# Both attentions in pairs of heads, the value product turned round, the weights divided before the transpose

## The chip, the cores and the metric

The kernel runs on one core of a Trainium2 chip. The metric is device time in microseconds (us), lower is better. The engines are called as in the profile: PE is the matrix engine (TensorE), DVE the vector engine, ACT the scalar engine, POOL is GpSimd, SP issues most DMAs. Each engine works through its own queue in a fixed order.

## The reference, cut to what matters

The network has two blocks on 512 tokens of 1024 features. The first block runs a banded attention with a relative bias beside an RWKV recurrence, twice in depth in the reference's loop over its layers; the second has an mLSTM beside a "forgetting" attention, and more layers that this change leaves alone. Both attentions have 8 heads of 64 features and are softmax(scores + bias) times the values:

```
def chunk_band_attention(q, k, v, rel_bias):
    ...
    scores = jnp.einsum('bnqhd,bnkhd->bnhqk', qc, kb).astype(jnp.float32) * (d ** -0.5)
    ...
    scores = jnp.where(valid[None, :, None, None, :], scores + bias[None, None], NEG_INF)
    p = jax.nn.softmax(scores, axis=-1)
    out = jnp.einsum('bnhqk,bnkhd->bnqhd', p.astype(vb.dtype), vb)

def forgetting_attention(q, k, v, f_pre):
    F = jnp.cumsum(jax.nn.log_sigmoid(f_pre.astype(jnp.float32)), axis=-1)
    ...
        logits = jnp.einsum('bhqd,bhkd->bhqk', qb, k).astype(jnp.float32) * scale + fq[..., :, None] - F[..., None, :]
        logits = jnp.where(kpos[None, :] <= qpos[:, None], logits, -jnp.inf)
        p = jax.nn.softmax(logits, axis=-1)
        return jnp.einsum('bhqk,bhkd->bhqd', p.astype(v.dtype), v)
```

## The kernel before

A static scheduler puts the instructions of all stages into one fixed order for each engine; nothing is decided at run time. Most of the work is dense products (`dense_A`, line L163, 128x512 results named psA, and `dense_B`, L281, psB), whose weights stream in by DMA on SP's queue and are split into a high and a low part on ACT (L132) and DVE (L133). The scheduler fills the waits of other stages with such dense products where PSUM banks allow: they live in a pool `mm` of two banks.

The first block's attention (`attention1`, from L1520) works on two halves of four heads each; the second block's (in `layer0`, from L901) does the same. `attention_heads` (L1552) walks units of one head and one query tile t of 128 rows; in unit t the keys have n = 128(t+1) columns. A unit is: the scores (L1569, tile pss; the head's 64 features lie in one row half of PE's array), in the second attention also a causal mask added by a bf16 product (L1571); on DVE the bias added with a running minimum of the negated sum (L1573, into sb); on ACT the exponential with its sum (L1575); t+1 transposes on PE (L1583, pspt); a copy out of PSUM on ACT or DVE in turn (L1586, L1588, pT); and t+1 value products (L1597, pso), which hold a 128x128 piece of pT in the array and move 64 columns of v. After a head's four units the result is multiplied by 1/sum (L1600, L1601), and for two heads together it is transposed to feature rows by `rows_to_T` (L941, psr, four transposes) and split in high and low parts (L318 on ACT, L319 on DVE). PE's order is: scores of unit u, transposes of u-1, values of u-2. PSUM: attention1 has two banks for pss and pspt together, layer0 four; pso has one bank in attention1, two in layer0.

In attention1 the RWKV mixer runs at the same time: during its first half of heads DVE also does the triangular solve (`wk`, L1396 and L1397, 15 dependent steps), during the second half the last recurrence steps (L1450 to L1494) and the group norm (products L1502 and L1506, ACT's logarithm and exponential L1509 and L1511 with a table load each, DVE L1515 and L1516) run.

The lines above are those of the kernel before. Its functions, and those that call them:

Of the kernel before, what the change touches and what calls it, by code (L numbers as in the profile page):

```python
# [17 lines left out]
S = 512  # L18
# [8 lines left out]
# ---- per-feature vectors, features on partitions: name -> number of 128-columns  # L27
# [61 lines left out]
class Halves:  # L89
    """a tile [128, 2, 8, 256] (token half, feature tile, token) as [128 features, 512 tokens] of one feature tile"""  # L90
# [12 lines left out]
class Builder:  # L103
# [155 lines left out]
    def dense_B(self, xk, w, col0, pp, tag="mm", width=512, toks=(0, 1, 2, 3), ps=None, chunks=None, low=None):  # L259
        """x W[:, col0:col0+width], tokens on partitions: {token tile: [128, width] PSUM view}; low: as in dense_A"""  # L260
# [46 lines left out]
    def mix_part(self, xk, w, pp):  # L307
        """column half 0: xN = ALPHA * xN + the part of the mixer's output that is ready"""
# [28 lines left out]
    def to_T(self, xn, n, pair, t, pp, tag, k0=0):  # L337
        """xn: [128 tokens, n*128] -> columns t of pair's tiles k0..k0+n, split"""
# [20 lines left out]
    # ------------------------------------------------------------ row vectors  # L359
# [12 lines left out]
    def rsqrt(self, out, src, n, scale, eps):  # L372
        """out = (scale * src + eps) ** -0.5 on [128, n] columns"""
# [21 lines left out]
    def ln_apply(self, x, st, g, b):  # L395
        """layer norm over 1024 features in place, eps 1e-5; st: bn_stats of the halves"""
# [19 lines left out]
    # ------------------------------------------------------------------ setup  # L416
# [48 lines left out]
    # ---------------------------------------------------------- block 1 mixer  # L465
    def block1_in(self, pool):
# [3 lines left out]
        with ExitStack() as es:  # L470
# [13 lines left out]
            # the tensor engine's clock rises only while it works  # L484
# [308 lines left out]
    def log1pexp_neg_abs(self, out, u):  # L793
        """out = ln(1 + exp(-|u|))"""
# [5 lines left out]
    # ---------------------------------------------------------------- layer 0  # L800
    def layer0(self):
# [3 lines left out]
        with ExitStack() as es:  # L805
            with ExitStack() as es2:
                lp = self.pool(es2, "l0")
                dr = es2.enter_context(self.tc.tile_pool(name="l0d", bufs=1, space=bass.MemoryType.DRAM))
                sel = self.selector(lp, "w", 4)
                one = lp.tile([96, 512], F32, name="one")  # L810
# [5 lines left out]
                # the first two heads' v, and gates: forget rows 0:4 (mLSTM), 32:36 and 64:68 (attention), input rows 96:100  # L816
# [17 lines left out]
                gu = lp.tile([128, 512], F32, name="gu")  # L834
                nc.scalar.activation(gu, pg, AF.Identity, bias=self.p("b_gate"))
                # mLSTM inputs
# [19 lines left out]
                F = lp.tile([96, 512], F32, name="F")  # L856
# [3 lines left out]
                nF = lp.tile([96, 512], F32, name="nF")  # L860
# [4 lines left out]
                cr = lp.tile([32, 512], F32, name="cr")  # L865
# [3 lines left out]
                M = lp.tile([32, 512], F32, name="M")  # L869
                nc.vector.tensor_tensor_scan(M, one[0:32, :], cr, 0.0, op0=ALU.mult, op1=ALU.max)  # L870
                em = lp.tile([32, 512], F32, name="em")
# [3 lines left out]
                # columns by token: c (0:4 of each 64), exp(-m) (32:36)  # L875
# [24 lines left out]
                idb = lb.tile([128, 128], BF16, name="idb")  # L900
                nc.vector.tensor_copy(idb, self.ident)  # L901
                cm = lb.tile([128, 128], BF16, name="cm")
                nc.gpsimd.memset(cm, 0.0)
                nc.gpsimd.affine_select(out=cm, in_=cm, pattern=[[-1, 128]], base=0, channel_multiplier=1, compare_op=ALU.is_ge, fill=NEG)
# [775 lines left out]
```

## Time and profile before

| | |
|---|---|
| median of 3 runs | 2110.13 us (2109.53 to 2110.42) |
| profiled execution, first to last instruction (span) | 2106.5 us |
| runs above that span | 3.0 to 3.9 us |
| PE busy | 2065.2 us (98%) |
| DVE, ACT, POOL busy | 1114.8, 765.6, 163.5 us |
| mean granted clock of PE | 0.995 |

The busy share of PE is a mean over the whole span, and a busy PE is not a PE at its peak: two products that use half of the array each count as busy whether they run one after the other or side by side. How long PE waits, and for whom, is read at each place.

### The profile page before, as it was taken

The numbers are of one execution on the slowest core, as the hardware profiler recorded it, in microseconds if no ns is written. First come the engines' busy times: TensorE is split into PE (matmuls) and PEld (weight loads), VectorE is DVE, ScalarE is ACT, GpSimd is POOL, SyncE is SP. The second block draws the span as 40 slices with busy tenths as digits, with TensorE's granted clock in tenths as the row PEclk, the third lists the DMA queues.
The fourth block names the chain that finished last, engine by engine and source line by source line (L and its number), as shares of the span: only waits on it lengthen the run. The fifth ranks groups of instructions, "written<-read, shape, count | busy, mean of one in ns | idle before, by whom it ended". The sixth has DMA issues, their size and how long they took to land.

```text
span 2106.5 us, 27707 instructions
## 1 busy us (share of the span) xinstructions
PE 2065.2 (98%) x11216; PEld 1696.1 (81%) x11216; DVE 1114.8 (53%) x1831; ACT 765.6 (36%) x1213; POOL 163.5 (8%) x258
## 2 busy tenths in 40 slices
PE   8999999999999999999999999999999999999998
PEld 6678677777888888888777888888897789888886
DVE  4554455565532424544534765435576676543565
ACT  4431552144333423333333344314334534432441
POOL 1101110110000000112200000000020310000000
PEclk9999999999999999999999999999999999999999
DMA  6241125143233334232212322333322033332332
GB/s 205 71 88 42 31 71 107 42 145 104 77 94 100 93 97 125 76 107 80 61 60 91 101 89 91 100 106 109 112 74 80 31 110 101 100 100 90 100 100 91
DMA packets 175120, 192.52 MB, mean 91 GB/s; under 512 B 31560, under 2 KB 144712, under 8 KB 174992
## 3 DMA queue, kind: packets, MB, share of 16 engines
q1 hardware_dynamic: 169920, 173.40, 27.4%
q0 software_dynamic: 5072, 17.35, 2.6%
q8 instruction: 88, 1.44, 0.3%
q14 instruction: 40, 0.33, 0.1%
HBM read 184.94 MB, written 5.78 MB: 91 GB/s over the span
## 4 chain that ended last, share of the span: by engine, by line
PE 53%; DVE 1%; DMA 1%; POOL 1%; ACT 0%; issue 0%; DVEq 0%; ACTq 0%; POOLq 0%
PE psA L163 29%; PE psB L281 19%; PE pss L1569 1%; PE pso L1597 1%; PE pho L1137 1%; DMA raw<-od_w_out 1%; PE psT L345 0%; PE pspt L1583 0%; PE ppg L1176 0%; PE pss L1571 0%; PE pqk L965 0%; PE pho L973 0%; DVE wlo L133 0%; PE psr L941 0%; ACT whi L132 0%
## 5 line engine op out<-in xcount | busy, mean ns | idle before, releaser
L133 DVE TENSOR_TENSOR wlo<-raw,whi 128x1024 fp32r<-128x1024 f32 (+1 forms) x295 | 360.3, 1224 | 506.9 <-ACT whi L132 303.3
L132 ACT ACTIVATE whi<-raw 128x1024 fp32r<-128x1024 f32 (+1 forms) x295 | 311.7, 1056 | 635.7 <-PE psA L163 288.4
L163 PE MATMUL psA<-xTh,whi 128*128 128x512 f32 (+1 forms) x1616 | 416.9, 378 | 3.6 <-ACT xTh L318 1.7
L163 PE MATMUL psA<-xTl,whi 128*128 128x512 f32 (+1 forms) x1616 | 415.8, 377 | 1.3 <-DVE st L375 1.3
L163 PE MATMUL psA<-xTh,wlo 128*128 128x512 f32 (+1 forms) x1616 | 412.1, 376 | 0.0
L163 PEld LDWEIGHTS psA<-xTh,whi 128*128 128x128 f32 x1616 | 288.8, 189 | 59.6 <-issue 3.0
L163 PEld LDWEIGHTS psA<-xTl,whi 128*128 128x128 f32 x1616 | 291.1, 190 | 56.2 <-issue 2.7
L163 PEld LDWEIGHTS psA<-xTh,wlo 128*128 128x128 f32 x1616 | 286.9, 188 | 53.3 <-issue 2.3
L772 DVE SCALAR_TENSOR_TENSOR v<-psA,par,v 128x511 f32<-128x511 f32 (+1 forms) x176 | 131.3, 747 | 78.9 <-ACT v L770 76.5
L376 POOL TENSOR_TENSOR st<-st,mhalf 128x1 f32<-128x1 f32 (+1 forms) x40 | 32.9, 822 | 1266.7 <-DVE st L375 1266.5
L281 PE MATMUL psB<-whi,hidh 128*128 128x512 f32 x480 | 126.7, 390 | 0.0
L281 PE MATMUL psB<-wlo,hidh 128*128 128x512 f32 x480 | 126.4, 389 | 0.0
L281 PE MATMUL psB<-whi,hidl 128*128 128x512 f32 x480 | 126.4, 389 | 0.0
L281 PEld LDWEIGHTS psB<-whi,hidl 128*128 128x128 f32 x480 | 90.1, 188 | 18.8
L281 PEld LDWEIGHTS psB<-wlo,hidh 128*128 128x128 f32 x480 | 90.1, 188 | 18.7
L281 PEld LDWEIGHTS psB<-whi,hidh 128*128 128x128 f32 x480 | 90.0, 188 | 18.7
L770 ACT ACTIVATE v<-psA,par 128x512 f32<-128x512 f32 x88 | 67.8, 771 | 98.0 <-PE psA L163 98.0
L281 PE MATMUL psB<-whi,xTh 128*128 128x256 f32 (+2 forms) x320 | 53.4, 289 | 0.0
L281 PE MATMUL psB<-whi,xTl 128*128 128x256 f32 (+2 forms) x320 | 52.6, 287 | 0.6 <-DVE xTl L319 0.6
L318 ACT ACTIVATE xTh<-psT 128x512 fp32r<-128x512 f32 x40 | 21.9, 595 | 84.2 <-PE psT L345 84.2
L281 PE MATMUL psB<-wlo,xTh 128*128 128x256 f32 (+2 forms) x320 | 49.3, 286 | 0.0
L1575 ACT ACTIVATE sb<-sb,sm 128x128 f32<-128x128 f32 (+1 forms) x64 | 35.7, 559 | 34.1 <-DVE sm L1573 33.5
(406 smaller groups left out, 2503.2 us busy)
## 6 DMA issues: line engine op xcount, KB each, us to landing
raw<-fup SPq DMA_DIRECT2D x88, 512.0 KB, 3.5
raw<-fdn SPq DMA_DIRECT2D x44, 512.0 KB, 3.3
raw<-w_in SPq DMA_DIRECT2D x42, 512.0 KB, 3.8
raw<-w_up SPq DMA_DIRECT2D x32, 512.0 KB, 3.8
raw<-w_down SPq DMA_DIRECT2D x32, 512.0 KB, 3.7
raw<-ev_w_in SPq DMA_DIRECT2D x26, 512.0 KB, 3.7
raw<-od_w_in SPq DMA_DIRECT2D x14, 512.0 KB, 3.8
raw<-w_out SPq DMA_DIRECT2D x8, 512.0 KB, 3.7
```

Of the source, the lines that this page charges most:

```text
L132: i = nc.scalar.activation(hi, raw, AF.Copy)
L133: self.w_ins = (i, nc.vector.tensor_tensor(lo, raw, hi.bitcast(F32), op=ALU.subtract))
L163: i = nc.tensor.matmul(o.rearrange("p (h t) -> p h t", h=2) if len(x.shape) == 3 else o, wt[:, k, fs], x, start=first and half != 1, stop= ...
L281: nc.tensor.matmul(ps[t], xk[k0 + k][a][:, t * 128 : t * 128 + 128], wt[:, k, :], start=first, stop=(end and k == kn - 1 and wt is lo), sk ...
L318: nc.scalar.activation(hi, src, AF.Copy)
L376: return nc.gpsimd.tensor_tensor(out, out, self.mhalf[:, 0:n], op=ALU.pow)
L770: nc.scalar.activation(v, ps[f], AF.Identity, scale=self.p(f"fcw{l}", 88 + ft), bias=self.p(f"fcb{l}", ft))
L772: nc.vector.scalar_tensor_tensor(v[:, sh:], ps[f][:, : 512 - sh], self.p(f"fcw{l}", tap * 44 + ft), v[:, sh:], op0=ALU.mult, op1=ALU.add)
L1137: nc.tensor.matmul(po[:, t, :], w[:, (t - j) * 128 : (t - j) * 128 + 128], xdt[j][:, h * 64 : h * 64 + 64], start=(j == 0 and t == 0), sto ...
L1569: nc.tensor.matmul(ps[:, 0:n], q[hs, t * 128 : t * 128 + 128], k[hs, 0:n], start=True, stop=cmask is None, skip_group_check=True)
L1575: nc.scalar.activation(sb[:, 0:n], sb[:, 0:n], AF.Exp, scale=-1.0, bias=sm[:, t : t + 1], accum_out=sm[:, 4 + t : 5 + t])
L1597: nc.tensor.matmul(po[:, t, :], pT[:, j * 128 : j * 128 + 128], v(j), start=(t == 0 and j == 0), stop=(j == t), skip_group_check=True)
```

## The change

The units are now a pair of heads and a query tile (`attention_pairs`).
- Both heads' scores are issued one behind the other in the two row halves of the array, each into a bank of its own (L1566). The score stage has the same bias and exponential instructions as before, two of each a unit (L1570, L1572).
- The exponentials are multiplied by 1/sum (reciprocal L1579) before they are transposed (L1581): the first head's tile on DVE, the second's on POOL. The multiplication of the result (L1601) is gone.
- The transposes (L1586) go, in attention1, into the two banks of `mm`, which the dense products also use; in layer0 into the four banks of `ax`. The copies are the first head's on ACT (L1589), the second's on DVE (L1591).
- The value product is turned round (L1604): v (128x64) is held, pT moves in 128 columns, and the two heads write the two column halves. The result has features on rows, so `rows_to_T` and its transposes are gone, and the split reads pso.
- The causal mask is put into the bias of the second attention ahead of time: per head four DMAs and four selections on POOL (L906, L908) instead of one DMA, three buffers instead of two. The bf16 mask products are gone.
- The tiles sb and pT of both attentions come from one ring of eight.

```diff
-                def fbias(h):
-                    b = lb.tile([128, 512], F32, tag="fb", bufs=2, name=self.nm("fb"))
-                    nc.gpsimd.dma_start(b, bass.AP(tensor=fd.tensor, offset=fd.offset + h * 512, ap=[[0, 128], [1, 512]]))
-                    return lambda t: b[:, 0 : 128 * (t + 1)]
+                def fbias(h):
+                    b = lb.tile([128, 1280], F32, tag="fb", bufs=3, name=self.nm("fb"))
+                    row = lambda t: b[:, 64 * t * (t + 1) : 64 * (t + 1) * (t + 2)]
+                    for t in range(4):
+                        nc.gpsimd.dma_start(row(t), bass.AP(tensor=fd.tensor, offset=fd.offset + h * 512, ap=[[0, 128], [1, 128 * (t + 1)]]))
+                        d = row(t)[:, t * 128 : t * 128 + 128]
+                        nc.gpsimd.affine_select(out=d, in_=d, pattern=[[-1, 128]], base=0, channel_multiplier=1, compare_op=ALU.is_ge, fill=NEG)
+                    return row
...
+        def scores(u):
+            ...
+            for e in range(2):
+                nc.tensor.matmul(ps[e][:, 0:n], q[hf[e], t * 128 : t * 128 + 128], k[hf[e], 0:n], start=True, stop=True)
+            for e in range(2):
+                b = tt("sb")
+                nc.vector.tensor_tensor_reduce(out=b[:, 0:n], in0=ps[e][:, 0:n], in1=bias[id(pr)][e](t), op0=ALU.add, op1=ALU.min,
+                                               scale=-1.0, scalar=3e38, accum_out=sm[:, e : e + 1])
+                nc.scalar.activation(b[:, 0:n], b[:, 0:n], AF.Exp, scale=-1.0, bias=sm[:, e : e + 1], accum_out=sm[:, 2 + e : 3 + e])
...
+        def weights(u):
+            nc.vector.reciprocal(sm[:, 2:4], sm[:, 2:4])
+            for e in range(2):
+                (nc.vector, nc.gpsimd)[e].tensor_scalar(sb[e][:, 0:n], sb[e][:, 0:n], sm[:, 2 + e : 3 + e], None, op0=ALU.mult)
+            for e in range(2):
+                pt = ptile(self.nm("pspt"))
+                for j in range(n // 128):
+                    nc.tensor.transpose(pt[:, j * 128 : j * 128 + 128], sb[e][:, j * 128 : j * 128 + 128], self.ident)
...
+        def values(u):
+            for j in range(t + 1):
+                for e in range(2):
+                    nc.tensor.matmul(o[hf[e], t * 128 : t * 128 + 128], v(j, e), pT[e][:, j * 128 : j * 128 + 128],
+                                     start=(t == 0 and j == 0), stop=(j == t), skip_group_check=True)
+            if t == 3:
+                self.split(o, *out)
```

How the order moves, at three places. First PE in the first half of attention1's heads, near its start: the rows before (psA are dense products, the numbers behind the names are buffers).

```order
L163 MATMUL psA_1738<-xTh_83,whi_1742 128x512 x4
L163 MATMUL psA_1738<-xTl_84,whi_1742 128x512
L1583 MATMUL pspt_1503<-start,sb_1495 128x128
L163 MATMUL psA_1738<-xTl_84,whi_1742 128x512 x2
L1569 MATMUL pss_1507<-qk_1367,qk_1301 128x384
L1583 MATMUL pspt_1512<-start,sb_1500 128x128 x2
L1597 MATMUL pso_1489<-v_1371,pT_1505 128x64
L163 MATMUL psA_1738<-xTl_84,whi_1742 128x512
```

And the rows of PE at the same place now.

```order
L1566 MATMUL pss_1504<-qk_1367,qk_1301 128x256
L1566 MATMUL pss_1505<-qk_1367,qk_1301 128x256
L1566 MATMUL pss_1526<-qk_1367,qk_1301 128x384
L1566 MATMUL pss_1527<-qk_1367,qk_1301 128x384
L1586 MATMUL pspt_1517<-start,sb_1497 128x128
L1586 MATMUL pspt_1521<-start,sb_1500 128x128
L1586 MATMUL pspt_1539<-start,sb_1508 128x128 x2
L1586 MATMUL pspt_1544<-start,sb_1511 128x128 x2
L1604 MATMUL pso_1549<-pT_1519,v_1371 64x128
```

The dense products that stood between the attention's steps, 39 in this half, now stand behind its last transposes and values. The second half of heads now stands behind the whole recurrence, with only the group norm's four products between its steps, and its 37 dense products stand behind it as well.

Second DVE in the second half of attention1's heads: what stood around the group norm's last four operations (yT) before.

```order
L1515 SCALAR_TENSOR_TENSOR yT_974<-yT_974,par,gsq_976 128x512
L1515 SCALAR_TENSOR_TENSOR yT_975<-yT_975,par,gsq_977 128x512
L1516 SCALAR_TENSOR_TENSOR yT_974<-yT_974,par,bon_574 128x512
L1516 SCALAR_TENSOR_TENSOR yT_975<-yT_975,par,bon_610 128x512
L1601 TENSOR_TENSOR o_1985<-pso_2031,sm_2030 128x4x64
```

And what stands there now.

```order
L1579 RECIPROCAL st_2008<-st_2008 128x2
L1513 SCALAR_TENSOR_TENSOR yT_974<-yT_974,par,gsq_976 128x512
L1513 SCALAR_TENSOR_TENSOR yT_975<-yT_975,par,gsq_977 128x512
L1514 SCALAR_TENSOR_TENSOR yT_974<-yT_974,par,bon_574 128x512
L1514 SCALAR_TENSOR_TENSOR yT_975<-yT_975,par,bon_610 128x512
L1581 TENSOR_SCALAR sb_2013<-sb_2013,st_2008 128x256
```

The multiplication of unit t=1's weights, which that unit's transposes on PE wait for, now stands behind the group norm's four operations.

Third POOL in the first half of the second attention's heads; before, POOL had only the bias DMAs there.

```order
L908 DMA fb_8442<-fd 128x512
L908 DMA fb_8504<-fd 128x512
L908 DMA fb_8845<-fd 128x512
L908 DMA fb_8891<-fd 128x512
```

Now the multiplications L1581 of the second head of each pair stand among the DMAs and selections of the later heads' biases (fb).

```order
L1581 TENSOR_SCALAR sb_8410<-sb_8410,st_8402 128x384
L906 DMA fb_8476<-fd 128x128
L906 DMA fb_8476<-fd 128x256
L906 DMA fb_8476<-fd 128x384
L906 DMA fb_8476<-fd 128x512
L1581 TENSOR_SCALAR sb_8437<-sb_8437,st_8429 128x512
L908 AFFINE_SELECT fb_8476<-fb_8476 128x128 x2
```

The multiplication of the first pair's last unit stands behind four DMA issues. On SP's queue only the place of two weight transfers of the second block's closing product changes.

## Rows read from the trace of the kernel before

**Rows 1.** Windows, only line L163 on PE: start and end, length, busy (count), clock, DMA.

```profile
119.94:156.65 36.71, 13.40 (x39) 1.00 0.47 95
213.19:260.94 47.75, 12.86 (x37) 1.00 0.12 34
1045.86:1080.63 34.77, 9.44 (x27) 1.00 0.16 46
1081.00:1096.00 15.00, 15.00 (x68) 1.00 0.35 106
```

**Rows 2.** Windows, only line L281 on PE, same columns.

```profile
1108.22:1141.00 32.78, 7.58 (x43) 1.00 0.18 57
```

**Rows 3.** Timeline of PE: start, duration, engine, line, operation, tiles, shapes, count.

```profile
1049.94 1.12 PE L1569 MATMUL pss<-k,q 64*128 64x512 f32 x2
...
1051.06 0.61 PE L1597 MATMUL pso<-fv,pT 128*128 128x64 f32 x4
1051.51 0.50 PE L1583 MATMUL pspt<-start,sb 128*128 128x128 f32 x3
1051.94 0.48 PE L1569 MATMUL pss<-k,q 64*128 64x128 f32 x2
...
1052.39 0.71 PE L163 MATMUL psA<-xTl,whi 128*128 128x512 f32 x2
```

**Rows 4.** Timeline of PE, recurrence inside the second attention stretch (first and last of 13).

```profile
214.04 0.43 PE L1488 MATMUL psy<-PR,S 128*128 128x64 f32 x2
...
227.68 0.45 PE L1494 MATMUL psy<-G,VW 128*64 128x64 f32 x8
```

**Rows 5.** Groups of PE by shape, 213 to 261: busy us, mean ns.

```profile
L1502 PE MATMUL psm<-yT,cst 128*128 128x512 f32 x4 | 2.1, 618 | 0.0
```

**Rows 6.** Timeline of PE, products with two row halves of the array.

```profile
103.07 1.32 PE L1369 MATMUL psg<-PR,KB 64*128 64x128 f32 x16
```

**Rows 7.** Groups of DVE by shape, 119.94 to 156.65: busy us, mean ns | idle before.

```profile
L1573 DVE CUSTOM_DVE_ANT_0 sb<-pss,relb 128x512 f32<-128x512 f32 x4 | 2.8, 692 | 2.3 <-PE pss L1569 2.3
...
L1573 DVE CUSTOM_DVE_ANT_0 sb<-pss,relb 128x128 f32<-128x128 f32 x4 | 1.2, 291 | 6.8 <-PE pss L1569 5.6 <-issue 1.2
L1600 DVE RECIPROCAL sm<-sm 128x4 f32<-128x4 f32 x4 | 0.7, 174 | 0.9 <-ACT sb L1575 0.9
```

**Rows 8.** Groups of DVE by line, the same stretch: the two lines of the solve.

```profile
L1396 DVE TENSOR_TENSOR wk<-wk 128x1 f32<-128x1 f32 (+14 forms) x15 | 4.5, 301 | 0.2
...
L1397 DVE TENSOR_REDUCE wk<-wk 128x1 f32<-128x1 f32 (+14 forms) x15 | 3.5, 236 | 0.3
```

**Rows 9.** Timeline of ACT: two exponentials in the second attention.

```profile
1114.65 0.71 ACT L1575 ACTIVATE sb<-sb,sm 128x512 f32<-128x512 f32 x1
...
1115.36 0.39 ACT L1575 ACTIVATE sb<-sb,sm 128x128 f32<-128x128 f32 x1
```

**Rows 10.** Groups of POOL by shape, whole span.

```profile
L1475 POOL TENSOR_SCALAR S<-S,eLC 128x128 f32<-128x128 f32 x24 | 15.6, 659 | 134.2 <-DVE S L1483 91.9 <-DVE S L1481 42.3
...
L1325 POOL TENSOR_TENSOR KB<-ta,eLm 128x512 f32<-128x512 f32 x4 | 5.9, 1483 | 17.1 <-DVE ta L1324 13.4 <-ACT VW L1351 3.7
...
L908 POOL DMA_DIRECT2D fb<-fd x8 | 4.4, 557 | 94.2 <-DVE sm L1573 93.2 <-DMA fd<-nF 1.0
...
L1444 POOL MEMSET gsq<- 128x512 f32 x4 | 2.1, 531 | 0.0
```

**Rows 11.** Timeline of ACT, DVE and PE around the group norm.

```profile
240.13 1.28 ACT L1511 ACT_TABLE_LOAD   x1
...
242.09 1.41 DVE L1515 SCALAR_TENSOR_TENSOR yT<-yT,par,gsq 128x512 f32<-128x512 f32 x2 [2.84 <-ACT gsq L1511]
...
243.28 0.44 PE L1583 MATMUL pspt<-start,sb 128*128 128x128 f32 x2 [1.90 <-ACT pT L1586]
```

**Rows 12.** Windows of 3 us on PE: busy (count), granted clock, DMA.

```profile
1632.00:1635.00 3.00, 1.18 (x5) 1.00 0.14 50
...
1638.00:1641.00 3.00, 3.00 (x9) 0.53 0.01 3
```

More of the change, by code (lines that the diff above doesn't have):

```diff
@@ L807, in layer0 @@
                 lp = self.pool(es2, "l0")
+                tt = lambda n, rows=128: lp.tile([128, 512], F32, tag="t", bufs=8, name=self.nm(n))[0:rows]
                 dr = es2.enter_context(self.tc.tile_pool(name="l0d", bufs=1, space=bass.MemoryType.DRAM))
                 sel = self.selector(lp, "w", 4)
-                one = lp.tile([96, 512], F32, name="one")
+                one = tt("one", 96)
                 nc.gpsimd.memset(one, 1.0)
@@ L855, in layer0 @@
                 self.po = self.pool(es2, "pspo", 2, psum=True)
-                F = lp.tile([96, 512], F32, name="F")
+                F = tt("F", 96)
                 self.log1pexp_neg_abs(F, gu[0:96, :])
@@ L1544, in attention1 @@
                 nc.scalar.activation(v[:, t, :], ps[t], AF.Copy)
-            o = [ap.tile([128, 4, 128], F32, tag="o", bufs=2, name=self.nm("o")) for _ in range(2)]
-            self.attention_heads(ap, [
-                (qk[0][hh // 2], qk[1][hh // 2], hh, lambda j, hh=hh, v=v: v[:, j, hh * 64 : hh * 64 + 64], o[hh // 2],
-                 lambda hh=hh: rbias(4 * hf + hh), None) for hh in range(4)])
-            for f in range(2):
-                self.rows_to_T(o[f], self.ya[0][:, 2 * hf + f, :], self.ya[1][:, 2 * hf + f, :])
@@ L1552, in attention_heads, with attention_pairs @@
-    def attention_heads(self, ap, heads):
+            self.attention_pairs(lambda n: ap.tile([128, 512], F32, tag="t", bufs=8, name=self.nm(n)), [
+                (qk[0][f], qk[1][f], lambda j, e, f=f, v=v: v[:, j, f * 128 + e * 64 : f * 128 + e * 64 + 64],
+                 lambda e, f=f, hf=hf: rbias(4 * hf + 2 * f + e), (self.ya[0][:, 2 * hf + f, :], self.ya[1][:, 2 * hf + f, :]))
+                for f in range(2)], lambda n: mm.tile([128, 512], F32, tag="mm", name=n))
+    def attention_pairs(self, tt, pairs, ptile):
@@ L1555, in attention_heads @@
         nc, at = self.nc, self.at
-        units = [(hd, t) for hd in heads for t in range(4)]
-        st = {}
+        units = [(pr, t) for pr in pairs for t in range(4)]
+        hf = (slice(0, 64), slice(64, 128))
+        st, po, bias = {}, {}, {}
         def scores(u):
-            hd, t = units[u]
-            q, k, h, v, o, biasf, cmask = hd
+            pr, t = units[u]
+            q, k, v, biasf, out = pr
             if t == 0:
-                sm = ap.tile([128, 8], F32, tag="sm", bufs=3, name=self.nm("sm"))
-                st[id(hd)] = (sm, self.po.tile([128, 4, 64], F32, tag="po", name=self.nm("pso")), biasf())
-            sm, po, bf = st[id(hd)]
-            hs = slice((h % 2) * 64, (h % 2) * 64 + 64)
+                bias[id(pr)] = [biasf(e) for e in range(2)]
@@ L1567, in scores @@
             n = 128 * (t + 1)
-            ps = at.tile([128, 512], F32, tag="ax", name=self.nm("pss"))
-            nc.tensor.matmul(ps[:, 0:n], q[hs, t * 128 : t * 128 + 128], k[hs, 0:n], start=True, stop=cmask is None, skip_group_check=True)
-            if cmask is not None:
-                nc.tensor.matmul(ps[:, n - 128 : n], cmask[0], cmask[1], start=False, stop=True, skip_group_check=True)
-            sb = ap.tile([128, 512], F32, tag="sb", bufs=3, name=self.nm("sb"))
-            nc.vector.tensor_tensor_reduce(out=sb[:, 0:n], in0=ps[:, 0:n], in1=bf(t), op0=ALU.add, op1=ALU.min,
-                                           scale=-1.0, scalar=3e38, accum_out=sm[:, t : t + 1])
@@ L1575, in scores @@
-            nc.scalar.activation(sb[:, 0:n], sb[:, 0:n], AF.Exp, scale=-1.0, bias=sm[:, t : t + 1], accum_out=sm[:, 4 + t : 5 + t])
-            st[u] = sb
-        def transposes(u):
-            n = 128 * (units[u][1] + 1)
-            sb = st[u]
-            pt = at.tile([128, 512], F32, tag="ax", name=self.nm("pspt"))
-            for j in range(n // 128):
-                nc.tensor.transpose(pt[:, j * 128 : j * 128 + 128], sb[:, j * 128 : j * 128 + 128], self.ident)
-            pT = ap.tile([128, 512], F32, tag="pT", bufs=2, name=self.nm("pT"))
-            if u % 2 == 0:
-                nc.scalar.activation(pT[:, 0:n], pt[:, 0:n], AF.Copy)
-            else:
-                nc.vector.tensor_copy(pT[:, 0:n], pt[:, 0:n])
-            st[u] = pT
@@ L1591, in values @@
-        def values(u):
-            hd, t = units[u]
-            h, v, o = hd[2:5]
-            sm, po, _ = st[id(hd)]
+            sm = self.stat(4)
+            ps = [at.tile([128, 512], F32, tag="ax", name=self.nm("pss")) for _ in range(2)]
+            for e in range(2):
+                nc.tensor.matmul(ps[e][:, 0:n], q[hf[e], t * 128 : t * 128 + 128], k[hf[e], 0:n], start=True, stop=True)
+            sb = []
+            for e in range(2):
[3 more added lines that the diff above has]
+                nc.scalar.activation(b[:, 0:n], b[:, 0:n], AF.Exp, scale=-1.0, bias=sm[:, e : e + 1], accum_out=sm[:, 2 + e : 3 + e])
+                sb.append(b)
@@ new lines, in scores @@
+            st[u] = (sb, sm)
+        def weights(u):
+            n = 128 * (units[u][1] + 1)
+            sb, sm = st[u]
+            nc.vector.reciprocal(sm[:, 2:4], sm[:, 2:4])
+            for e in range(2):
+                (nc.vector, nc.gpsimd)[e].tensor_scalar(sb[e][:, 0:n], sb[e][:, 0:n], sm[:, 2 + e : 3 + e], None, op0=ALU.mult)
+            row = []
+            for e in range(2):
+                pt = ptile(self.nm("pspt"))
+                for j in range(n // 128):
+                    nc.tensor.transpose(pt[:, j * 128 : j * 128 + 128], sb[e][:, j * 128 : j * 128 + 128], self.ident)
+                pT = tt("pT")
+                if e == 0:
+                    nc.scalar.activation(pT[:, 0:n], pt[:, 0:n], AF.Copy)
+                else:
+                    nc.vector.tensor_copy(pT[:, 0:n], pt[:, 0:n])
+                row.append(pT)
+            st[u] = row
@@ L1595, in values @@
+        def values(u):
+            pr, t = units[u]
+            v, out = pr[2], pr[4]
+            if t == 0:
+                po[id(pr)] = self.po.tile([128, 512], F32, tag="po", name=self.nm("pso"))
+            o = po[id(pr)]
             pT = st.pop(u)
             for j in range(t + 1):
-                nc.tensor.matmul(po[:, t, :], pT[:, j * 128 : j * 128 + 128], v(j), start=(t == 0 and j == 0), stop=(j == t), skip_group_check=True)
+                for e in range(2):
+                    nc.tensor.matmul(o[hf[e], t * 128 : t * 128 + 128], v(j, e), pT[e][:, j * 128 : j * 128 + 128],
+                                     start=(t == 0 and j == 0), stop=(j == t), skip_group_check=True)
@@ L1607, in attention_heads @@
             if 1 <= u <= n:
-                transposes(u - 1)
+                weights(u - 1)
             if u >= 2:
```

36 lines of the change are left out of this document (13 added, 23 removed).

## The prediction

> **What bounds the kernel now.** I read the page's shares first: PE is busy for 98% of the span, and the chain of waits runs almost throughout along PE's dense products. The metric is the length of PE's queue, waits included; what other engines save counts only where PE waits for them. Next I read windows for the dense products alone around the four stretches of attention [rows 1, 2], for there the scheduler lays dense work between the attention's steps. A dense psA product takes 15.00/68 = 0.22 us, a psB of half the columns 0.11. A stretch minus its dense products is what the attention itself costs; I call it the net. First attention, first half: 36.71 - 39 x 0.22 = 28.1, and 0.6 for the four feature-row transposes that come later, 28.7. Second half: 47.75 - 37 x 0.22 = 39.6, minus 5.9 for the recurrence between the steps (its pieces, from 214.04 to 228 [rows 4]), plus 0.6: 34.3. Second attention: 34.77 - 27 x 0.22 = 28.8, and 32.78 - 43 x 0.11 + 1.1 (eight later transposes) = 29.2. Together 121.0. In these nets PE hardly waits, since the dense work stands under every chain of the softmax; the one long wait is 1.90 us in the group norm [rows 11].
>
> **What goes.** The timeline of PE [rows 3] gives each step as the distance to the next start: scores with mask 1.12 (512 columns) and 0.45 (128), so without the mask (I take off 0.05) about 1.06 and 0.41, 0.22 for each further 128; four value products 0.45, or 0.112 each; three transposes 0.43, or 0.143 each. The masks, half of the value work and the feature-row transposes go, and the scores of two heads run at once, if row halves do that. The trace shows that they do: eight products (16 instructions) with 64 rows and 128 columns, in alternating row halves, take 1.32 [rows 6], where eight scores of that size one by one would take 8 x 0.41 = 3.3.
>
> **What comes.** PE's work for a pair of heads, W: scores 0.41 + 0.63 + 0.84 + 1.06 = 2.95; transposes 20 x 0.143 = 2.86; value products, ten pairs of 128 columns. For column halves the trace has no row: side by side 0.225 (twice 0.112, twice the columns), one after the other 0.45. I take 0.27, nearer the row halves' case, so 2.7. W = 8.5.
>
> Against that stands a longer chain, C, from a unit's scores to the transposes of its second head: two bias additions on DVE (0.29 at 128 columns to 0.69 at 512 each [rows 7]), the second head's exponential (0.39 to 0.71 [rows 9], and 0.1 for reading its sum, an estimate), the reciprocal (0.17 [rows 7]), POOL's multiplication, and 0.2 for hand-overs (my estimate). POOL's multiplication of 128 columns is in the trace, 0.66; of 512 it is not [rows 10]. Below, it grows as DVE's addition does, by 0.13 for each 128 columns: 1.06, which a memset of 512 columns (0.53) does not exclude. Above, it is proportional: 2.64. The nearest row is the operation of two inputs on 512 columns, 1.48; with one input I take 1.40. C is then 2.1, 2.7, 3.3 and 4.0 for the four tiles, 12.1 a pair.
>
> The order on PE is scores of u, transposes of u-1, values of u-2. The transposes of u+1 start C behind the scores of u+1, and these stand behind the transposes of u-1 and the values of u-2. So two units take C + W, and a pair (12.1 + 8.5)/2 = 10.3; two pairs 20.6. The ends add the first score (0.4) and the last unit's transposes, copy and values (8 x 0.143 + 0.6 + 4 x 0.27 = 2.8): **23.8 for a half**. PE waits in it, since the dense work that stood there now stands behind it: in attention1 the transposes take the two banks that the dense products need.
>
> - Second attention: each half 23.8, and 0.7 because a multiplication stands behind four DMA issues of 0.557 each [rows 10] (between 0, if they are early, and 2.2): 24.5. That is 4.3 and 4.7 less than before.
> - First attention, first half: DVE also has the solve, 4.5 + 3.5 = 8.0 [rows 8]. Bias additions (3.9 a pair), reciprocals (0.7), its multiplications and copies (estimate: 3) leave it about 2.7 free in 10.3. Before, the solve lay under dense work; now I let three quarters of it, 6.0, delay the additions that PE waits for (0 if it fits in, 8.0 at most). 1.0 more where the next pair's values wait for the split of the single pso bank (ACT and DVE, 512 columns each, by [rows 7, 9] 0.7 each, part of it hidden): 30.8, or 2.1 more.
> - Second half: 23.8, the group norm's products (2.1 for four instructions [rows 5], and four more alike, 4.2), 1.0 as above, and a wait. Logarithm and exponential with two table loads are 2 x (1.28 + 0.71) = 4.0 on ACT, then four DVE operations of 0.70 [rows 11] = 2.8, and the multiplication of t=1 stands behind these: 6.8, less 0.8 of products that PE has ready: 6.0. Behind the multiplication are queued that unit's transposes, then all of PE. 35.0, or 0.7 more. What is late next is the weight split for the following dense products, which has room: DVE is busy for half of the span.
> [...]
>
> At nothing I set: the two exchanged weight transfers on SP (weights come some us ahead of their products), the bias rows of the first pair (issued long before, under dense work), the ring of eight (a unit needs four), the third bias buffer. If the bias of the later pairs is late, that is the 2.2 above.
>
> Sum: 2.1 + 0.7 - 4.3 - 4.7 + 1.5 = -4.7 on the span of 2106.5, 2101.8; the runs lie 3.6 above that span at the median: **2105.5**.
>
> [...]
>
> **Rivals.**
> - *Quick multiplication* (1.06 at 512 columns): 0.7 less a half, 2102.5. For it: the memset. Against: the row of 1.48.
> - *Slow multiplication* (2.64, proportional): C grows by 2.5 a pair, a half by 2.5, in all 10: 2115.5, **slower**. For it: 0.66 for only 128 columns; against: 1.48 for four times as many with two inputs. It turns the gain into a loss from about 2.0 at 512 columns, into a measurable one from 2.5.
> - *The clock falls again and again*: in the first attention PE works for 17 of 31 us in a half, in pieces. [...] For it: [rows 12]. Against: over the whole second half, with its wait of 1.90, the clock was 1.00 [rows 1].
> - *The halves do not run side by side* (the change does not do what it says): scores 2.95 and values 2.65 more a pair, so W + 5.6, half of it in the period, 5.6 a half: 2128. Against: [rows 6]; but column halves have no row.
>
> [...]
>
> **How the numbers follow.** A difference of 0.2% (4.2 us) is about what a measurement of this kernel can tell from none. Chances: forecast 0.42, with a range of its own of 2101.5 to 2109.5 (value products 0.225 to 0.45: -2 to +7 at the ends, solve 0 to 8.0: -6 to +2); quick 0.15; slow 0.17; clock 0.18; one after the other 0.08. Faster (under 2105.9): quick and half of the forecast, 0.37. Same: the other half, and the milder third of slow and clock that ends under 2114.4, 0.27. Slower: 0.36. Leaving out the serial case and the tails of the others, the range is 2099 to 2119.
>
> **What would show it.** In the changed profile: pairs of scores whose second starts far less than its own length behind the first, at 512 columns together near 1.1; the row of POOL's multiplication at 512 columns near 1.4; PE's transposes waiting for POOL in every unit, some 1.5 to 2 at t=3; nets of the second attention near 24.5, of the first near 31 and 35; one wait of some 4 to 6 us in the group norm; the granted clock lower in at most one short place. Wrong it would be if the multiplication costs over 2.0, if the clock is below 1.00 through an attention, if DVE's additions come more than 6 us late through the solve, or if dense weights come late because the attention now holds DVE and ACT without pause.

## The result, and the profile after

The changed kernel runs at 2131.78 us (median of 4, 2124.37 to 2133.82), the kernel before beside it at 2110.28: 1.0095 times as long by the means of the runs, with an interval of 1.0082 to 1.0109. It is slower by about 1%; forecast were 2105.5 us, and the range ended at 2119. The profiled execution is the quickest of the four, with a span of 2122.7 us against 2106.5; the other three have lower mean clocks (0.978 to 0.981 against 0.985) and are longer.

The first place to look is where the span grows. I bound each attention by two products of its neighbourhood that are the same in both kernels: from the first to the last Gram product of the recurrence for the first attention, and from the last mLSTM product to the first prefix-sum product of the layer behind for the second. Windows of PE, kernel before: start and end, length, busy time (count), granted clock, DMA.

```profile
103.10:327.50 224.40, 220.27 (x1611) 1.00 0.24 61
1018.90:1575.30 556.40, 555.77 (x2911) 1.00 0.30 93
```

The same two of the changed kernel.

```profile
104.60:345.70 241.10, 222.25 (x1596) 0.93 0.23 56
1039.70:1592.70 553.00, 542.68 (x2864) 1.00 0.33 97
```

The second attention is 3.4 us shorter, the first 16.7 longer, and the mean clock there is 0.93 in place of 1.00. The other 2.9 of the span's 16.2 lie outside both: 1.5 more ahead of the first, 2.6 more between them, 1.2 less behind. (Between them the change also moves seven tiles of the second block's gates and mLSTM, `one`, `gu`, `F`, `nF`, `cr`, `M` and `em`, into the ring of eight; PE's wait for ACT's q at 947 us is 2.8 us there in place of 2.0.) PE's idle time in the first stretch is 241.1 - 222.3 = 18.9 us, before 4.1. Windows of 5 us of the changed kernel, PE, same columns, show where the clock goes, and three of 1 us where it turns.

```profile
120.00:125.00 5.00, 3.83 (x25) 1.00 0.36 52
125.00:130.00 5.00, 4.51 (x19) 0.66 0.31 100
130.00:135.00 5.00, 3.46 (x21) 0.82 0.32 105
135.00:140.00 5.00, 5.00 (x29) 0.50 0.02 5
140.00:145.00 5.00, 3.37 (x25) 1.00 0.00 0
...
235.00:240.00 5.00, 0.21 (x2) 0.90 0.00 0
240.00:245.00 5.00, 2.98 (x11) 0.50 0.00 0
245.00:250.00 5.00, 5.00 (x26) 0.50 0.19 52
250.00:255.00 5.00, 5.00 (x21) 0.50 0.00 0
255.00:260.00 5.00, 5.00 (x19) 0.50 0.00 0
260.00:265.00 5.00, 4.17 (x23) 0.71 0.00 0
...
130.00:131.00 1.00, 0.80 (x10) 1.00 0.00 0
133.00:134.00 1.00, 0.49 (x3) 0.59 0.90 361
239.00:240.00 1.00, 0.00 (x0) 0.50 0.00 0
```

0.50 is the lowest clock in any window of 1 us of both kernels; I call it the lower level. By windows of 1 us it is there three times (I call each a fall): from about 126 to 130 and from 133 to 140 us, after pieces of waiting of less than a microsecond each, and from 239, within one wait of 6.49 us (235.2 to 241.7), to 263, over 20 us after the wait although PE is busy almost throughout. Products take longer there. Sixteen instructions of value products, timeline of PE:

```profile
254.17 1.97 PE L1604 MATMUL pso<-pT,v 128*64 128x128 f32 x16
```

From their start to the next product's, at 256.08, are 1.91 us; at a clock of 1.00 sixteen take 1.33 (below, at 1142.73) or 1.25 (in b2, described below, at 246.69). All of it counts as busy, so the busy time hides the loss. What PE waited for, whole span: engine, line, waited-for line, us, times, longest.

```profile
PE pspt L1586 <- DVE sb L1581: 10.7, 10, 6.5
PE pspt L1586 <- POOL sb L1581: 8.6, 12, 1.7
...
PE pss L1566 <- DVE st L1570: 2.5, 6, 0.8
```

Before, the attentions had one such wait of 1.90 us [rows 11]. The multiplications, groups by shape, on POOL and (last row) on DVE:

```profile
L1581 POOL TENSOR_SCALAR sb<-sb,st 128x512 f32<-128x512 f32 x8 | 13.7, 1708 | 6.0 <-DVE st L1579 5.9
L1581 POOL TENSOR_SCALAR sb<-sb,st 128x384 f32<-128x384 f32 x8 | 10.5, 1315 | 19.0 <-DVE st L1579 18.9
L1581 POOL TENSOR_SCALAR sb<-sb,st 128x256 f32<-128x256 f32 x8 | 8.2, 1026 | 4.9 <-DVE st L1579 4.6
L1581 POOL TENSOR_SCALAR sb<-sb,st 128x128 f32<-128x128 f32 x8 | 6.4, 796 | 89.6 <-DVE st L1579 62.5 <-DVE wk L1395 27.1
...
L1581 DVE TENSOR_SCALAR sb<-sb,st 128x512 f32<-128x512 f32 x8 | 4.5, 559 | 0.2
```

POOL takes 0.80 us at 128 columns and 1.71 at 512, where DVE takes 0.56, a third of it. The products of two heads overlap, though not everywhere as far as costed. Timeline of PE in the second half of the second attention, where every window shows a clock of 1.00:

```profile
1134.36 1.37 PE L1566 MATMUL pss<-k,q 64*128 64x512 f32 x4
1135.65 0.65 PE L1604 MATMUL pso<-pT,fv 128*64 128x128 f32 x6
...
1142.73 1.39 PE L1604 MATMUL pso<-pT,fv 128*64 128x128 f32 x16 [0.30 <-ACT pT L1589]
1144.06 0.39 PE L281 MATMUL psB<-whi,y2l 128*128 128x256 f32 x1
```

Two scores of 512 columns take 1.29 us from start to next start, where the prediction reads 1.06 for one and takes the same for two; four pairs of value products (16 instructions) 1.33, so 0.33 a pair against 0.27 taken, 0.225 if fully side by side and 0.45 if one followed the other. At the same clock other places have 1.19 and 1.54 (b2, 128.40 and 141.42 us) for such a pair of scores and 1.25 for the sixteen: the halves run side by side in part, and no run shows what decides how far.

The prediction counted in nets, a stretch of attention less its dense products. The four stretches of the changed kernel, all of PE:

```profile
121.45:154.58 33.13, 26.81 (x155) 0.85 0.33 69
226.17:271.58 45.41, 35.09 (x161) 0.74 0.06 18
1066.68:1100.18 33.50, 28.22 (x176) 0.95 0.43 78
1128.97:1158.10 29.13, 25.41 (x189) 1.00 0.30 47
```

In them are 2, 2, 23 and 0 dense products L163 and 1, 1, 1 and 37 L281. At 0.22 and 0.11 us each the nets are 32.6, 44.9, 28.3 and 25.1, where 30.8, 35.0, 24.5 and 24.5 were forecast. The second half of the first attention misses by the most, 9.9 us.

### The profile page after: what moved, and what is told of

The parts are those of the page before. It is cut to its first block, busy times and chain, and to the rows that moved or that the text cites. A ratio compares the mean times of both kernels' runs of the same rounds, so it can differ in the third digit from the quotient of the medians.

```text
span 2122.7 us, 27739 instructions
## 1 busy us (share of the span) xinstructions
PE 2055.6 (97%) x11152; PEld 1681.0 (79%) x11152; DVE 1118.9 (53%) x1862; ACT 766.2 (36%) x1213; POOL 221.4 (10%) x344
## 4 chain that ended last, share of the span: by engine, by line
PE 50%; POOL 1%; DVE 1%; DMA 1%; issue 1%; ACT 1%; DVEq 0%; POOLq 0%; ACTq 0%; SPq 0%
PE psA L163 29%; PE psB L281 19%; PE pho L1135 1%; DMA fb<-fd 1%; PE psT L345 1%; POOL sb L1581 0%; POOL fb L906 0%; PE pho L971 0%; PE pqk L963 0%; DMA raw<-fup 0%; PE pso L1604 0%; PE pss L1566 0%; ACT sb L1572 0%; DMA raw<-ev_w_out 0%; POOL ho L1002 0%
## 5 line engine op out<-in xcount | busy, mean ns | idle before, releaser
L163 PE MATMUL psA<-xTh,whi 128*128 128x512 f32 (+1 forms) x1616 | 416.0, 378 | 2.5 <-ACT xTh L318 1.9
L163 PE MATMUL psA<-xTl,whi 128*128 128x512 f32 (+1 forms) x1616 | 414.1, 377 | 1.3 <-DVE st L375 1.3
L163 PE MATMUL psA<-xTh,wlo 128*128 128x512 f32 (+1 forms) x1616 | 409.8, 376 | 0.0
L163 PEld LDWEIGHTS psA<-xTh,whi 128*128 128x128 f32 x1616 | 289.3, 189 | 60.1 <-issue 3.9
L163 PEld LDWEIGHTS psA<-xTl,whi 128*128 128x128 f32 x1616 | 292.1, 190 | 55.9 <-issue 1.6
L163 PEld LDWEIGHTS psA<-xTh,wlo 128*128 128x128 f32 x1616 | 287.9, 189 | 54.3 <-issue 2.0
L281 PE MATMUL psB<-whi,hidh 128*128 128x512 f32 x480 | 126.7, 390 | 0.0
L281 PE MATMUL psB<-wlo,hidh 128*128 128x512 f32 x480 | 126.5, 389 | 0.0
L281 PE MATMUL psB<-whi,hidl 128*128 128x512 f32 x480 | 126.4, 389 | 0.0
L281 PEld LDWEIGHTS psB<-whi,hidl 128*128 128x128 f32 x480 | 90.1, 188 | 18.8
L281 PEld LDWEIGHTS psB<-wlo,hidh 128*128 128x128 f32 x480 | 90.1, 188 | 18.8
L281 PEld LDWEIGHTS psB<-whi,hidh 128*128 128x128 f32 x480 | 89.9, 188 | 18.7
L281 PE MATMUL psB<-whi,xTl 128*128 128x256 f32 (+2 forms) x320 | 53.1, 288 | 0.6 <-DVE xTl L319 0.6
L281 PE MATMUL psB<-whi,xTh 128*128 128x256 f32 (+2 forms) x320 | 53.3, 289 | 0.0
L1586 PE MATMUL pspt<-start,sb 128*128 128x128 f32 x160 | 32.1, 323 | 20.2 <-DVE sb L1581 10.7
L1581 POOL TENSOR_SCALAR sb<-sb,st 128x128 f32<-128x128 f32 (+3 forms) x32 | 38.7, 1211 | 119.5 <-DVE st L1579 91.9
```

The source lines that it names most:

```text
L163: i = nc.tensor.matmul(o.rearrange("p (h t) -> p h t", h=2) if len(x.shape) == 3 else o, wt[:, k, fs], x, start=first and half != 1, stop= ...
L281: nc.tensor.matmul(ps[t], xk[k0 + k][a][:, t * 128 : t * 128 + 128], wt[:, k, :], start=first, stop=(end and k == kn - 1 and wt is lo), sk ...
L1581: (nc.vector, nc.gpsimd)[e].tensor_scalar(sb[e][:, 0:n], sb[e][:, 0:n], sm[:, 2 + e : 3 + e], None, op0=ALU.mult)
L1586: nc.tensor.transpose(pt[:, j * 128 : j * 128 + 128], sb[e][:, j * 128 : j * 128 + 128], self.ident)
```

## The experiments

Three theories stood against each other: (1) the loss is PE's clock, which falls because PE has no dense work under its waits in the first attention; (2) the loss is the waits for the divided weights themselves, POOL's above all; (3) products in array halves lower the clock by themselves. Every kernel ran beside the kernel before on the same chip. The table gives medians and, from one profile each, the two stretches bounded as above (rows of several of them follow). A stretch is thus one execution's, which need not be the median: a2's took 2099.8 us, b1's 2106.4.

| kernel | us | ratio to before, interval | first stretch, clock | second stretch |
|---|---|---|---|---|
| before | 2110.3 to 2111.8 | | 224.4, 1.00 | 556.4 |
| changed | 2131.8 | 1.0095 (1.0082 to 1.0109) | 241.1, 0.93 | 553.0 |
| a1 | 2112.2 | 1.0004 (0.9990 to 1.0018) | 224.6, 1.00 | 553.4 |
| a2 | 2105.6 | 0.9969 (0.9958 to 0.9980) | 219.4, 1.00 | 552.0 |
| a3 | 2116.9 | 1.0046 (1.0017 to 1.0075) | 232.1, 0.96 | 556.6 |
| a4 | 2115.0 | 1.0016 (1.0003 to 1.0029) | 228.2, 1.00 | 553.5 |
| b1 | 2102.3 | 0.9955 (0.9941 to 0.9968) | 224.8, 0.98 | 544.1 |
| b2 | 2108.1 | 0.9993 (0.9977 to 1.0009) | 228.7, 0.98 | 543.8 |
| b3 | 2125.4 | 1.0065 (1.0052 to 1.0078) | 232.7, 0.98 | 555.4 |
| b4 | 2107.3 | 0.9980 (0.9969 to 0.9990) | 219.4, 1.00 | 556.5 |
| c1 | 2091.6 | 0.9908 (0.9890 to 0.9925) | 215.6, 1.00 | 542.4 |
| c2 | 2101.5 | 0.9953 (0.9937 to 0.9969) | 221.8, 1.00 | 544.0 |
| c3 | 2117.4 | 1.0036 (1.0019 to 1.0052) | 231.0, 0.96 | 554.2 |

**a1: only the second attention changed** (the first has the functions of the kernel before).

> Only the second attention is changed, the first is as in the kernel before. Theory 1 (the changed kernel lost its time through the lower level of PE's clock in the first attention: windows show 0.85 over 33.1 us, 0.74 over 45.4 us, that is 5.0 + 11.8 us): the second attention's own gain of 3 to 5 us stays, 2104 to 2108 us, clock near 0.99. Theory 2 (the waits for the divided weights themselves cost the time, wherever they stand): the second attention has 8 us of such waits, so 2110 to 2118 us.

2112.2 us, no difference from before. Theory 2's number came, but not for its reason: the second attention saves 3.0 us in its stretch, as theory 1 said, although PE waits there 8.3 us for weights (6.1 of them POOL's). The profiled span is 4.2 us longer all the same, since the lower level also comes outside both stretches: for some 31 us in this execution, 17 in the one of the kernel before (windows of 1 us). One such place, first before, then a1, in both behind a wait of 1.78 us for the same DVE result (L1327 and, in a1, L1325, tile ta) and with the same products next:

```profile
85.00:90.00 5.00, 5.00 (x21) 1.00 0.00 0
...
85.00:90.00 5.00, 5.00 (x10) 0.50 0.00 0
```

So a gain or a loss of a few us in a median can be a matter of such falls.

**a2: the first attention's transposes in the scores' banks.**

```diff
-                for f in range(2)], lambda n: mm.tile([128, 512], F32, tag="mm", name=n))
+                for f in range(2)], lambda n: self.at.tile([128, 512], F32, tag="ax", name=n))
```

> The first attention's transposes take the banks of its scores, not the two of the dense products; pairs, division and everything else as changed. The dense products then stand between its steps again. Theory 1: the clock stays at 1.00 in both halves, 2100 to 2110 us. Theory 2: the waits for the weights are covered too, but scores wait for the transposes' banks, 2105 to 2115 us. Theory 3 (products in row and column halves side by side bring the clock down by themselves): the clock falls again in the first attention, over 2120 us.

2105.6 us, 26 less than the changed kernel, by one line. Dense psA products stand between the attention's steps again, as its timeline of PE shows; behind it PE's windows of the two stretches:

```profile
121.16 0.49 PE L1566 MATMUL pss<-qk,qk 64*128 64x128 f32 x4
121.58 0.73 PE L163 MATMUL psA<-xTh,whi 128*128 128x512 f32 x2
122.25 0.70 PE L1566 MATMUL pss<-qk,qk 64*128 64x256 f32 x4
...
104.30:323.70 219.40, 214.63 (x1595) 1.00 0.25 61
1016.00:1568.00 552.00, 541.22 (x2864) 1.00 0.33 97
```

The first stretch has pairs, POOL's multiplication and a clock of 1.00: theory 3 falls. Idle time is 4.8 us in place of 18.9.

**a3: the kernel before, with the transposes in the dense products' banks.**

```diff
-            pt = at.tile([128, 512], F32, tag="ax", name=self.nm("pspt"))
+            pt = at.tile([128, 512], F32, tag="ax", name=self.nm("pspt")) if at is self.ax else self.mm.tile([128, 512], F32, tag="mm", name=self.nm("pspt"))
```

> The kernel before (heads one by one, division at the end), with one edit: in the first attention the transposes take the banks of the dense products. No pair, no POOL multiplication. Theory 1: PE waits in small pieces and the clock falls in the first attention, 2120 to 2140 us. Theories 2 and 3: the clock stays at 1.00 and only the uncovered chain of one head shows, 2112 to 2122 us.

2116.9 us: below theory 1's range, within the other's, so the time alone doesn't decide. The windows do: without any pair the clock falls to the lower level in the second half, behind a wait of 3.04 us in the group norm, while the first half, whose chain of one head is shorter, stays at 1.00.

```profile
240.00:245.00 5.00, 1.96 (x9) 0.84 0.00 0
245.00:250.00 5.00, 3.90 (x16) 0.50 0.01 3
250.00:255.00 5.00, 5.00 (x12) 0.50 0.00 0
255.00:260.00 5.00, 5.00 (x26) 0.50 0.00 0
```

**a4: useless products under the waits.** `ident` seen as bf16, into the banks that the transposes then overwrite.

```diff
                 pt = ptile(self.nm("pspt"))
+                if at is not self.ax:
+                    self.nun = getattr(self, "nun", 0) + 1
+                    for _ in range(56 if self.nun == 19 else 2 if self.nun % 2 else 4):
+                        nc.tensor.matmul(pt[:, 0:256], warm[:, 0:128], warm, start=True, stop=True)
```

> The changed kernel, with bf16 products of no use (128x256, some 0.11 us each; 2 ahead of the first head's transposes, 4 ahead of the second's, 56 ahead of those that wait behind the group norm) in the banks of the first attention's transposes, which then overwrite them: about 16 us of PE work added, most of it under waits. The result is the reference's. Theory 1: the clock stays near 1.00 there and the time falls to 2112 to 2122 us although work was added. Theory 2: nothing that PE waits for comes earlier, 2132 to 2145 us.

2115.0 us: 17 less with more work. PE's window of the first stretch:

```profile
106.00:334.20 228.20, 220.95 (x1746) 1.00 0.24 59
```

The clock is 1.00 and the stretch 12.9 us shorter. No wait was taken away (the multiplications are the same), but PE is idle in the stretch for 7.3 us in place of 18.9: this part of the loss is the clock, which fell where PE's waits stood open and not here, where they are filled.

**b3: such products only behind the group norm** (56 there, none elsewhere).

> The changed kernel with 56 useless bf16 products (128x256) ahead of the transposes that wait behind the group norm, and none elsewhere; the result is the reference's. Theory 1: the clock stays at 1.00 in the second half of the first attention (11.8 us were lost there) and falls in the first half as before (5.0 us lost): 2117 to 2123 us. Theory 2: no change or slower, 2130 to 2140 us.

2125.4 us, just above theory 1's range. In the second half the clock is 1.00; it falls in the first half, now at 140 to 155 us (0.72, 0.50, 0.76). So the falls of the two halves are separate, each with its own waits. The first half's products are those of the changed kernel, whose clock fell there at 126 and 133: where the falls come is not the same in every execution.

**b2: both multiplications on DVE.**

```diff
-                (nc.vector, nc.gpsimd)[e].tensor_scalar(sb[e][:, 0:n], ...)
+                nc.vector.tensor_scalar(sb[e][:, 0:n], ...)
```

> The changed kernel, with both multiplications on DVE, the transposes in the dense products' banks as changed. Theory 1 (the clock): the waits shrink by some 5 us but PE still has no dense work in the first attention, the clock falls there again, 2122 to 2131 us. Theory 2 (POOL's slow multiplication is the loss): 2108 to 2118 us, near the kernel before.

2108.1 us: theory 1's number was wrong by 14 us, theory 2's right. PE's windows:

```profile
230.00:235.00 5.00, 2.02 (x13) 0.92 0.00 0
235.00:240.00 5.00, 2.42 (x12) 0.50 0.00 0
240.00:245.00 5.00, 4.67 (x26) 0.56 0.16 52
```

With shorter waits (the longest is 4.5 us, for ACT's copy in the group norm) the clock holds at 1.00 through the first half, and in the second it recovers within 12 us. The transposes still stand in the dense products' banks. So in the first attention POOL's multiplication was a cause of the falls: (1) and (2) are two links of one chain there, not rivals, as I had set them. In the second attention it is a loss of its own, as c3 shows.

**c3: DVE's multiplication in the first attention only** (POOL's in the second).

> The changed kernel, with both multiplications on DVE in the first attention only; the second attention keeps POOL's. Both changed to DVE gave 2108.1 us, the changed kernel 2131.8. If the loss is all in the first attention, where no dense product stands under the waits: 2108 to 2114 us. If POOL's share is spread over both attentions: 2115 to 2125 us.

2117.4 us. POOL's share is spread: the second attention's stretch is 554.2 us here and 543.8 in b2, so POOL's multiplication costs 10 us there, at a mean clock of 0.99 to 1.00. Two short falls of this execution are in the 10 us (0.66 at 1075 to 1080 us, 0.75 and 0.90 up to 1090), worth 2 to 3 us (estimate: by these clocks some 7 us at the lower level, of which a third is lost, as in the changed kernel's first attention, or half, as the clock of 0.50 says). The first attention's part is the 14 us by which this kernel is below the changed one.

**b1: a2 with both multiplications on DVE.**

> As a2_pt_own_banks, with both multiplications of a pair on DVE, none on POOL. There PE still waited 6.2 us for POOL's multiplications (1.71 us at 512 columns in the changed kernel, DVE 0.49) and 2.7 us for DVE's. If POOL's share of the chain is what is left of the cost: 2.5 to 4 us less, 2101 to 2103 us. If DVE, which then has all of the softmax but the exponential, becomes what PE waits for: 2105 to 2110 us.

2102.3 us, the number of the first case, but out of two parts that neither case had. PE's windows of the stretches:

```profile
104.30:329.10 224.80, 218.79 (x1597) 0.98 0.23 60
1020.50:1564.60 544.10, 539.61 (x2865) 1.00 0.33 98
```

Against a2 the second attention gains 8 us, and the first loses 5 in this execution: a wait of 2.54 us in the group norm for DVE's bias addition, then the lower clock from 246 to 257. So DVE did become what PE waits for, as the second case said, and the sum fell into the first case's range by luck.

**c2: b1 with 24 useless products at that wait.**

> As b1_own_banks_dve, with 24 useless bf16 products (128x256, 2.6 us) ahead of the transposes of the second pair that waited 2.5 us behind the group norm, after which the clock was granted 0.61, 0.50 and 0.86 over 15 us (some 5 us lost); the result is the reference's. Theory 1 (the clock): 1.00 throughout the first attention, 2098 to 2102 us. If the clock's fall costs little there or comes anyway: 2102 to 2106 us.

2101.5 us, within theory 1's range but not to be told from b1. The clock is 1.00 in the whole first attention and its stretch 3 us shorter; in the median of all runs it does not show; that other falls hide it (the mean clocks of its runs go from 0.987 to 0.995) is likely and not shown.

**b4: a2's first attention alone** (second as before).

> Only the first attention is changed, with its transposes in the banks of its scores; the second attention is that of the kernel before. If the gain of a2_pt_own_banks (4.9 us) is all the first attention's, since a1_second_only gave no gain: 2104 to 2107 us. If the two parts each give some: 2107 to 2111 us.

2107.3 us, at the border of both ranges. Its first stretch, 219.4 us, is a2's; that a2 is 1.6 us quicker is within what the intervals leave open, and agrees with a1.

**c1: a2 with the second head's multiplication on ACT.**

```diff
-                (nc.vector, nc.gpsimd)[e].tensor_scalar(sb[e][:, 0:n], ...)
+                if e == 0:
+                    nc.vector.tensor_scalar(sb[e][:, 0:n], sb[e][:, 0:n], sm[:, 2 + e : 3 + e], None, op0=ALU.mult)
+                else:
+                    nc.scalar.activation(sb[e][:, 0:n], sb[e][:, 0:n], AF.Copy, scale=sm[:, 2 + e : 3 + e])
```

> As b1_own_banks_dve, but the second head's multiplication on ACT instead of DVE. b1 ran at 2102.3 us. If DVE is what the chain waits for there (PE waited 3.8 us for DVE's multiplications): 2098 to 2102 us. If ACT, which has the exponentials, the copies and in the group norm the table loads, delays the chain more: 2103 to 2108 us.

2091.6 us (2091.05 to 2092.95), below both ranges, and 19 us quicker than the kernel before: the best version. PE's windows and its largest wait on the attentions' weights:

```profile
104.60:320.20 215.60, 211.90 (x1596) 1.00 0.26 62
1013.20:1555.60 542.40, 538.80 (x2865) 1.00 0.34 99
```
```profile
PE pspt L1589 <- DVE sb L1582: 2.6, 4, 0.7
```

ACT's multiplication of 512 columns takes 0.71 us, more than DVE's 0.49 in b2; but it no longer stands in DVE's queue, and no wait of an attention is over 0.7 us. Of the stretches' gain against b1, 9.2 us lie in the first attention, whose clock is 1.00 without any useless product, and 1.7 in the second.

## Why the prediction was wrong

**The clock's term failed.** The 1.5 us in the sum, one fall of the clock behind the group norm's wait, is shown by no run; what the runs show in its place is three falls in the first attention of the profiled execution, of some 3, 7 and 24 us, together some 34 at the lower level, most of it (239 to 263 us) in and behind that wait. What they cost the first stretch can be read against c1, which issues the same products at a clock of 1.00: PE is busy for 211.9 us there, 222.3 in the changed kernel, so 10.3 us (7.6 by a2's 214.6). The other terms of the 16.7 us are idle time, up by 14.7, and the PE work that the change takes away, 220.3 - 211.9 = 8.4; that the three add up is how they are defined and proves nothing. The proof is a4: with every wait left in place, filling them took 12.9 us off the stretch.

The rival "the clock falls again and again" came nearest. A microsecond at the lower level cost about 0.3 (10.3 of 34, in part of which PE waits). My 1.5 was an estimate from [rows 12], half of three microseconds at the end of an unrelated wait, whose length I took for that of any fall. Against that rival I held that the clock was 1.00 in the kernel before through its 1.90 us wait; but there dense products stood on either side.

**The cover was seen, its price was not.** The text said that in attention1 the transposes take the dense products' banks and that dense work stands behind. It costed this as uncovered chain. That the missing cover also takes the clock with it is what a2 (26 us from one line) and a4 show, both at 1.00 in the first attention where the changed kernel has 0.93.

**POOL's multiplication was mis-sized**: 1.71 us at 512 columns against 1.40, 0.80 at 128 against 0.66. By the prediction's own period, (C + W)/2, the four differences (0.14 + 0.13 + 0.17 + 0.31 = 0.75 a pair, half of it in the period) give 0.75 a half, 3 us in all. The period underrates it. In the second attention, POOL's 0.80 + 1.03 + 1.32 + 1.71 against DVE's two multiplications one behind the other (2 x (0.29 + 0.35 + 0.46 + 0.49) = 3.2) is 1.7 a pair longer, 3.3 for four pairs, and with the 0.7 a half for the DMA issues on POOL's queue 4.7; measured are 7.9 (a2 to b1) and 10.4 (c3 to b2). So the second attention's forecast gain of 9.0 became 3.4. Some of the rest lies in the clock of 0.89 and 0.77 from 1085 to 1095 us; what else POOL's queue holds back there, with 32 DMA issues and 32 selections between the multiplications, no run separates.

**The sum of the miss.** The forecast span was 2101.8 us, the measured one 2122.7. Of these 20.9 us the clock in the first attention is 8.8 (10.3 in place of 1.5), the second attention 5.6, the rest of the first attention 3.6 and the places outside both 2.9; the last two have no cause shown. (By a4's 12.9 the clock is 11.4 and the rest of the first attention 1.0.) The median lies another 5.4 us further off. The range ended 13 us too low because each rival stood in it alone, while the clock and the multiplication came together.

**Right were** that the halves overlap (0.33 a pair of value products against 0.27), and the group norm's wait (6.49 us against 6.0), with its place: the multiplication of t=1 behind four DVE operations. The wait's size is in part luck: it holds 1.0 us by which that multiplication was longer than others of its size (last section), which the sum did not have, and PE had more products ready than the 0.8 taken off. Not needed was the wait for the solve: PE waited 2.1 us for bias additions in the first half, not 6.0. So the first half's net, 32.6 against 30.8, is near its forecast by luck too: 10 us at the lower level stand in it in place of that wait.

**Slips in the working.** In the rival with one half after the other, the value products are 10 x (0.45 - 0.27) = 1.8 a pair more, not 2.65; that rival is then some 2124.5 and not 2128. The milder third of the rivals "slow" and "clock" has a chance of 0.12, not 0.06, so that "same" is 0.33 and "slower" 0.31. Neither moves the forecast.

What stays open: when a fall comes and how long it lasts. Behind the same wait of 1.78 us the clock fell in a1 and not in the kernel before; in the group norm it stayed low for 24 us in the changed kernel, 17 in a3 and 10 in b1 and b2. The other three runs of the changed kernel are 6 to 9 us longer than the profiled one; their mean clocks point to more time at the lower level, but no trace shows where. The same holds for two of a3's ten runs (2136 and 2141 us, mean clocks 0.979 and 0.977) and two of b2's eleven (2121, 0.981).

## What to carry to other kernels

Before you give a stage's banks to something else, ask which work of other stages stood in that stage's waits: here it hid not only the chain but also kept the matrix engine's clock up (1.00 in a2's first attention, 0.93 in the changed kernel's), and the price of losing it was a fall that lasted over 20 us after a wait of 6.49. Do not put a new elementwise step of the chain on an engine only because its busy share is the lowest: moving one multiplication from POOL to ACT, beside DVE's, made a2 14 us quicker. Price a step on POOL by a row of its own kind and size; if there is none, keep the slow end as the likeliest.

## What the runs showed of the hardware

Two of DVE's multiplications took longer while POOL worked. In the changed kernel they took 1.35 and 1.24 us where those of their size take 0.35 and 0.42, and each ended 0.2 to 0.4 us behind the end of one of two POOL multiplications (2.97 us for both; by an estimate of half each, at 241.28 and 242.77). Timeline of DVE, then of POOL.

```profile
240.29 1.35 DVE L1581 TENSOR_SCALAR sb<-sb,st 128x256 f32<-128x256 f32 x1
...
241.76 1.24 DVE L1581 TENSOR_SCALAR sb<-sb,st 128x384 f32<-128x384 f32 x1
```
```profile
239.80 2.97 POOL L1515 TENSOR_TENSOR yb<-yT,g 128x512 f32<-128x512 f32 x2 [5.08 <-DVE yT L1514]
```

From POOL's first end, by that estimate, to the end of DVE's first row are 0.36 us, that row's usual length; from POOL's second end to the end of DVE's second row 0.23, less than a whole 0.42. What held the two back no row shows. The means differ in the same direction: DVE's multiplication of 512 columns takes 0.56 us in the changed kernel, where POOL has the other head's, and 0.49 in b2, where it has none.

The lower clock stayed over fully busy windows: from 245 to 260 us PE was busy for 15 of 15 us at 0.50, and in a4, whose products fill the wait ahead, the clock was 1.00 in every window of 5 us from 230 to 265.
